# Output projection of a GLA layer on one NeuronCore: fourteen instead of ten weight pairs multiplied by seven block products, with the weight sums regrouped

## The chip, the cores and the metric

The kernel runs on one core of one Trainium2 chip. The metric is the device time of one launch in microseconds (us); lower is better. Three runs of the kernel before took 1044.53, 1044.98 and 1045.18 us (median 1044.98). A separate, profiled execution gives the trace that is read here.

The engines are named as the profile names them: PE is TensorE's matmul stream and PEld its weight loads, DVE is VectorE, ACT is ScalarE, POOL is GpSimd, SP issues most of the DMAs.

## What is computed

One layer with batch 1, 256 tokens, width 2048: RMSNorm, a gated linear attention mixer with four heads, a residual add, RMSNorm, a squared-ReLU MLP of width 8192, a residual add, and a last RMSNorm, all in float32.

```python
h = x
h = h + _gla_mixer(_rmsnorm(h, gla_norm), w_in, w_gate_up, b_gate, o_norm, w_out)
h = h + _sq_relu_mlp(_rmsnorm(h, mlp_norm), w_up, w_down)
return _rmsnorm(h, final_norm)

def _gla_mixer(...):
...
    return (o * silu(r)) @ w_out          # the output projection, 2048 x 2048

def _sq_relu_mlp(h, w_up, w_down):
    a = relu(h @ w_up)
    return (a * a) @ w_down
```

The change lies in the output projection (`@ w_out`) and, with the regrouped sums alone, in the second MLP matmul (`@ w_down`).

## The kernel before

**Precision by splitting.** PE multiplies in fp32r. Each float32 operand is therefore split into a part `hi` (an ACT cast, `copy_hi`, L112 to L118) and a remainder `lo = raw - hi` (a DVE subtraction, L131 for weights as loaded, L761 and L1129 for sums of weights). One block product is three matmuls: x_hi by w_hi, x_lo by w_hi, x_hi by w_lo.

**Steps of the output projection.** `out_group` (L699) runs four times, for g = 0 to 3, each for 512 of the 2048 output columns. A group takes eight steps, one for each pair kp of 128-row weight tiles (256 rows in all), in the order of `ORDER` (L782). The step's weights are four blocks of 128 by 256: row tile i, column half. The activations of the pair are four blocks A11, A12, A21, A22 of 128 tokens by 128 rows: the first digit is the half of the tokens, the second the row tile.

- A *plain* step multiplies all eight block pairs: 8 products of 3 matmuls, 24 matmuls of 256 columns (L748).
- A *summed* step uses Winograd's scheme with seven products, 21 matmuls: four with sums of activations S1 to S4 and with sums of weights, and the rest with the blocks themselves. Three products use weight blocks as loaded (L740, 9 matmuls, here called the step's *raw product*); four use sums or follow them (L762 to L765, 12 matmuls, the *sums product*). The sums product is held back as `pending` and runs one step later, after that step's own products (L749).

Which steps are summed: `summed(g)` (L784), in groups 0 and 3 the pairs 0 and 1, in groups 1 and 2 the pairs 0, 1 and 7, ten steps in all.

**What a summed step needs.** (1) The two row tiles are loaded by SP's queue (L729), and POOL's queue then adds the second block onto the first by an accumulating DMA (L730). (2) The raw product casts and splits only 768 of the 1024 columns (L733). (3) DVE forms the other sums in place by three subtractions or additions of 128 by 256 (L743 to L745), after the split of the same step. (4) The result is cast by ACT in two pieces of 512 columns (L758, recorded at L118) and split by DVE (L761). (5) The activations must be there in *forms*, the eight blocks S1 to S4 and A11 to A22 side by side: `turn_pair` (L600) builds them from transposed blocks, with `form_sums` (L591, three DVE operations, recorded at L606), one ACT cast of 1024 columns (L607) and one DVE split (L608). A pair without forms goes the plain way of `turn` (L628 to L630). `FORMED` (L596) names the pairs that get forms.

**Banks.** A group accumulates its plain results in two PSUM banks, `banks[0]` and `banks[1]`, one for each half of the tokens, which begin as a copy of h (`begin_out`, L669). The summed products go to two more banks, `p16` and `p57`, which are the same physical banks in every group. After the last summed step of a group (`final`), ACT copies both to SBUF (`comb`, L767 and L768), DVE combines them (L769 to L772), and at the end of the group DVE adds `comb` and the plain banks into h (L775). The next group's first matmul into `p16` starts that bank afresh, so it must wait for the copy of L767.

**Order on the engines.** `then_mm` (L692) keeps the products in the written order on PE: each block of matmuls is issued after the last matmul of the block before it. `issue_after` orders casts and splits likewise. In what remains, the tile scheduler chooses the order. Weights live in `raw` buffers (six) and in five pairs of `hi` and `lo` slots (`slots`, L120); the raw product and the sums product of a summed step each take a slot pair. A cast waits until PE has finished with the slot pair five uses earlier.

**Work between the steps.** `between` (L785 to L795) places other work after a step: after step 1 the transposes of the previous group's finished h (`turn`, L610; L616 on PE, L629 on ACT, L630 on DVE), after step 3 the opening copies of the next group (L673), after step 4 the sums of squares (L780). In group 0, step 1 carries the transposes of the attention output's pairs 4 to 7 instead.

**The MLP.** `down` (L1019) uses the same seven products for nearly all pairs of `w_down`, 112 summed steps, alternating on PE with plain steps of `w_up`. Its sums are at L1088 to L1090, its casts at L1121, its split at L1129; `early` and `late` (L1130, L1131) are the two halves of the sums product, with matmuls of `w_up` between them.

Of the kernel before, what the change touches and what calls it, by code (L numbers as in the profile page):

```python
# [30 lines left out]
ALU = mybir.AluOpType  # L31

P = 128
T = 256
# [12 lines left out]
G = 1024  # L47
GT = 512
# [11 lines left out]
OFF = 48  # L60
# [8 lines left out]
def tile_gla_mlp(ctx, tc, x, xt, cols, w_vg, w_in, w_gate, w_out, w_up, w_down, final_norm, out):  # L69
    nc = tc.nc  # L70
# [515 lines left out]
                nc.scalar.activation(s, acc[t][c], AF.Silu, scale=r1[:, t : t + 1])  # L586
                nc.vector.tensor_tensor(on[:, t, lo : lo + 512], on[:, t, lo : lo + 512], s, op=ALU.mult)

    S3, S1, S2, S4, A12, A11, A22, A21 = range(8)

    def form_sums(f, sub):  # L591
        sub(f[:, S3 : S1 + 1], f[:, A21:].to_broadcast([P, 2, P]), f[:, A11 : A22 + 1])
        sub(f[:, S2], f[:, A11], f[:, S1])
        sub(f[:, S4], f[:, A12], f[:, S2])

    FORMED = (0, 1, 7)  # L596
    in_forms = lambda a: a.rearrange("p (f s) -> p f s", f=8)
    raw_forms = [in_forms(some[:, 4:6].rearrange("p a b -> p (a b)")), in_forms(mid.tile([P, G], F32, tag="db", name="form"))]

    def turn_pair(kp, bank, gain, to):  # L600

        raw_form = raw_forms[kp == 1]
        for i in range(2):
            s = bank[:, i * T : (i + 1) * T].rearrange("p (t s) -> p t s", t=NT)
            nc.scalar.activation(raw_form[:, A12 + 1 - i :: 2], s, AF.Copy, scale=gain(2 * kp + i))
        form_sums(raw_form, lambda o, x, y: nc.vector.tensor_tensor(o, x, y, op=ALU.subtract))  # L606
        nc.scalar.copy(to[0], raw_form)  # L607
        nc.vector.tensor_tensor(to[1], raw_form, to[0].bitcast(F32), op=ALU.subtract)  # L608

# [30 lines left out]
    def forms_o(kp):  # L640
        if kp < 2:
            return [of_pairs[:, kp, i] for i in range(2)]
        return [a[:, OFF : OFF + G].rearrange("p (f s) -> p f s", f=8) for a in (oth, otl)]

    def place_o(kt):

# [52 lines left out]
    def out_group(g, order, summed, between):  # L699

        tt = nc.vector.tensor_tensor
        banks = [out_banks[g, t] for t in range(NT)]
        sums_banks = []
        begun = set()
        pending = None
        block = lambda i, n=1: slice(i * T, (i + n) * T)

        def product(bank, o, a, w, n, last=False):
            for x in a[: 2 - n]:
                for d in range(0, w.shape[-1], T):  # L710
                    newest[0] = nc.tensor.matmul(
                        bank[:, o + d : o + d + T], x, w[:, d : d + T],
                        start=bank in sums_banks and bank.name not in begun, stop=last, skip_group_check=True,
                    ).ins
                    begun.add(bank.name)

        def products(these, w, last=False):
            with then_mm():
                for n in range(2):
                    for bank, o, a, c in these:  # L720
                        product(bank, o, a, w[n][:, c], n, last and n == 1)

        for step, kp in enumerate(order):
            by = kp in summed
            raw = raw_tile()[:, : 2 * GT]
            src = w_out[2 * kp * P : 2 * (kp + 1) * P, g * GT : (g + 1) * GT].rearrange("(i p) c -> p i c", p=P)
            if by:
                for i in range(2):
                    last_load[0] = nc.sync.dma_start(out=raw[:, i * GT : (i + 1) * GT], in_=src[:, i])  # L729
                nc.gpsimd.dma_start(out=raw[:, :T], in_=src[:, 0, T:], accum_op=ALU.add)  # L730
            else:
                last_load[0] = nc.sync.dma_start(out=raw.rearrange("p (i c) -> p i c", i=2), in_=src)
            w = parts(raw, 2 * GT, slots(), [(T * by, 2 * GT)])  # L733
            if by:
                if not sums_banks:
                    sums_banks.extend(psum_bank(i) for i in out_ids[4:])
                f = forms_o(kp)
                at = lambda k, f=f: [a[:, k] for a in f]
                p16, p57 = sums_banks
                products([(p16, 0, at(A11), block(1)), (banks[0], T, at(A12), block(3)), (banks[0], 0, at(S4), block(2))], w)  # L740
                u = raw.rearrange("p (f s) -> p f s", f=4)
                with tc.issue_after(last_lo[0].ins):
                    tt(u[:, 2], u[:, 0], u[:, 2], op=ALU.add)  # L743
                    tt(u[:, 1], u[:, 2], u[:, 1], op=ALU.subtract)
                    last = tt(u[:, 3], u[:, 2], u[:, 3], op=ALU.add)  # L745
            else:
                for t, i in ((0, 0), (0, 1), (1, 0), (1, 1)):
                    products([(banks[t], 0, row_o(2 * kp + i, t), block(2 * i, 2))], w, step == len(order) - 1 and i == 1)  # L748
            if pending:  # L749
                pending()  # L750
                pending = None
            if step in between:
                with tc.issue_after(last_hi[0].ins), tc.issue_after(last_lo[0].ins), then_mm():
                    between[step]()
            if by:
                def pending(u=raw, at=at, final=kp == [k for k in order if k in summed][-1]):
                    to = slots()
                    for c in (0, GT):  # L758
                        copy_hi(to[0][:, c : c + GT], u[:, c : c + GT])
                    with tc.issue_after(last_lo[0].ins):  # L760
                        last_lo[0] = tt(to[1][:, :G], u, to[0][:, :G].bitcast(F32), op=ALU.subtract)  # L761
                    products([  # L762
                        (p57, 0, at(S1), block(0)), (p57, T, at(S3), block(1)),
                        (p16, T, at(S2), block(2)), (banks[1], T, at(A22), block(3)),
                    ], to, final)  # L765
                    if final:
                        nc.scalar.copy(comb[:, 1:3], two(p16))  # L767
                        nc.scalar.copy(comb[:, 0:4:3], two(p57))  # L768
                        tt(comb[:, 2], comb[:, 1], comb[:, 2], op=ALU.subtract)  # L769
                        tt(comb[:, 0], comb[:, 0], comb[:, 2], op=ALU.subtract)  # L770
                        tt(comb[:, 4], comb[:, 0], comb[:, 3], op=ALU.add)
                        tt(comb[:, 5], comb[:, 2], comb[:, 3], op=ALU.subtract)  # L772
        for t in range(NT):
            o = h[:, t, g * GT : (g + 1) * GT].rearrange("p (f s) -> p f s", f=2)
            tt(o, two(banks[t]), comb[:, 4 * t : 4 * t + 2], op=ALU.add)  # L775

    def ssq_h(g):
# [144 lines left out]
    def on_vector(i):  # L922
        newest_form[1] = i.ins
# [30 lines left out]
    def forms(m, kp, s):  # L954
# [2 lines left out]
            f[:, A12:].rearrange("p (t i) s -> p i t s", t=2), s.rearrange("p i (t s) -> p i t s", t=2), AF.Square  # L957
        ))
        if True in ways_of(m, kp):
            form_sums(f, lambda o, x, y: on_vector(nc.vector.tensor_tensor(o, x, y, op=ALU.subtract)))  # L960

    def form_parts(m, kp, act):
        ways = ways_of(m, kp)
# [55 lines left out]
    def down(passes):  # L1019
# [7 lines left out]
        for n, (m, g) in enumerate(passes):  # L1027
# [12 lines left out]
            for kp in range(KP):  # L1040
# [40 lines left out]
                if by_parts:  # L1081
                    these = (P16, 0, at(A11), block(1)), (B32, T, at(A12), block(3)), (B32, 0, at(S4), block(2))
                    u = raw.rearrange("p (f s) -> p f s", f=4)
                    tt = nc.vector.tensor_tensor


                    with tc.issue_after(last_lo[0].ins):
                        tt(u[:, 2], u[:, 0], u[:, 2], op=ALU.add)  # L1088
                        tt(u[:, 1], u[:, 2], u[:, 1], op=ALU.subtract)  # L1089
# [19 lines left out]
                def of_sums(u=raw, products=products, at=at, kp=kp, banks=banks, quick=fresh and quick, g=g, then=ahead_of):  # L1109
# [11 lines left out]
                    for c in (0, GT):  # L1121
                        copy_hi(to[0][:, c : c + GT], u[:, c : c + GT])
                    if quick and kp == 0:
                        settle(P57)
                        banks[BX4] = begin(BX4, g)
# [41 lines left out]
    def combine(g):  # L1167
# [4 lines left out]
        def put(t):  # L1172
# [1 line left out]
            nc.vector.tensor_tensor(hv, hv, e[:, :2], op=ALU.add)  # L1174

        return [
            tt(2, 1, 2, ALU.subtract), tt(0, 0, 2, ALU.subtract), lambda: put(0),
            tt(1, 2, 3, ALU.subtract), tt(0, 0, 3, ALU.add), lambda: put(1),
        ]

    passes = [(m, g) for m in range(ROUNDS) for g in order_of(m) if m < ROUNDS - 1 or g < 2]
# [130 lines left out]
```

## Time and profile before

| | before |
|---|---|
| runs, us | 1044.53, 1044.98, 1045.18 |
| the profiled execution: its time, us | 1045.44 |
| its span, first to last instruction, us | 1043.7 |
| matmuls on PE | 9064 |
| granted PE clock, mean | 0.998 |
| DVE / ACT / POOL busy, share of the span | 83% / 69% / 11% |
| output projection on PE (L711), us from the span's start | 288.1 to about 376.6 |
| DMA throughput, mean | 217 GB/s |

The profile's page gives busy time by engine, then groups of instructions. Instruction rows in a timeline are "start, duration, engine, line, operation, output<-inputs, shape, count", with the idle time of the engine before it and what ended that in brackets. A row with a count covers several instructions in sequence: its duration runs from the first start to the last end. Two facts matter for reading it. Matmuls overlap, so PE's speed is read from the distance between starts, not from the busy share. DVE and ACT instructions overlap by some tens of ns too, so what one costs in a dense sequence is again the distance between starts.

### The profile page before, as it was taken

How to read it: one execution, taken by the hardware profiler on the slowest of the kernel's cores; microseconds unless marked ns; L12 is line 12 of the kernel's file. 1: busy time of each engine (PE TensorE's matmuls, PEld its weight loads, DVE VectorE, ACT ScalarE, POOL GpSimd, SP SyncE). 2: the span in 40 equal slices, each digit the busy share in tenths (PEclk: the TensorE clock that was granted, in tenths of full speed). 3: DMA queues.
4: the chain of work that ended last, by engine and by line, in shares of the span. 5: the costliest groups of instructions: out<-in, count | busy, mean ns of one | idle time of the engine just before them, and what ended most of it. 6: DMA issues, size and time to landing. Idle time of an engine off the chain costs nothing. (4 is left out here: it accounts for less than half of the span.)

```text
span 1043.7 us, 23272 instructions
## 1 busy us (share of the span) xinstructions
PE 1035.2 (99%) x9064; PEld 1034.3 (99%) x9064; DVE 871.1 (83%) x1287; ACT 721.7 (69%) x1084; POOL 117.8 (11%) x161
## 2 busy tenths in 40 slices
PE   9999999999999999999999999999999999999997
PEld 9999999999999999999999999999999999999997
DVE  5768644656498866889999999999999999999887
ACT  6785544546477755678678688778778777777785
POOL 0000000010011001111111111111111111111100
PEclk9999999999999999999999999999999999999999
DMA  9957665556666686678887887887888888887782
GB/s 333 334 174 208 197 195 170 152 152 182 175 204 189 209 256 190 179 210 226 228 247 230 236 235 217 239 236 223 246 232 222 249 230 228 231 227 225 233 244 89
DMA packets 118414, 226.53 MB, mean 217 GB/s; under 512 B 10608, under 2 KB 26864, under 8 KB 118176
## 3 DMA queue, kind: packets, MB, share of 16 engines
q1 hardware_dynamic: 100064, 207.39, 63.5%
q0 software_dynamic: 17568, 16.00, 10.3%
q8 instruction: 71, 1.16, 0.4%
q10 hardware_dynamic: 672, 1.66, 0.4%
q14 instruction: 39, 0.32, 0.1%
HBM read 222.91 MB, written 2.10 MB: 216 GB/s over the span
## 5 line engine op out<-in xcount | busy, mean ns | idle before, releaser
L118 ACT CAST hi<-raw 128x512 fp32r<-128x512 f32 (+4 forms) x630 | 499.5, 835 | 263.0 <-DVE raw L1089 73.0
L131 DVE TENSOR_TENSOR lo<-raw,hi 128x768 fp32r<-128x768 f32 (+3 forms) x226 | 238.7, 1061 | 90.9 <-ACT hi L118 88.4
L855 PE MATMUL acc<-hi,act 128*128 128x256 f32 x1696 | 247.9, 276 | 0.0
L855 PE MATMUL up<-hh,hi 128*128 128x256 f32 x1024 | 238.8, 277 | 0.0
L855 PE MATMUL up<-hl,hi 128*128 128x256 f32 x1024 | 238.7, 276 | 0.0
L165 DVE TENSOR_TENSOR lo<-raw,hi 128x1024 fp32r<-128x1024 f32 x160 | 195.0, 1221 | 29.9 <-ACT hi L118 29.5
L855 PEld LDWEIGHTS acc<-hi,act 128*128 128x128 f32 x1696 | 217.7, 188 | 0.0
L855 PEld LDWEIGHTS up<-hl,hi 128*128 128x128 f32 x1024 | 192.3, 188 | 0.0
L855 PEld LDWEIGHTS up<-hh,hi 128*128 128x128 f32 x1024 | 192.3, 188 | 0.0
L1065 POOL DMA_DIRECT2D raw<-in_w_down x112 | 97.1, 867 | 518.6 <-DMA raw<-in_w_down 229.8
L1129 DVE TENSOR_TENSOR lo<-raw,hi 128x1024 fp32r<-128x1024 f32 x112 | 136.7, 1220 | 1.3 <-ACT hi L118 1.0
L855 PE MATMUL up<-hh,lo 128*128 128x256 f32 x1024 | 137.0, 276 | 0.0
L855 PE MATMUL acc<-lo,act 128*128 128x256 f32 x848 | 134.1, 276 | 0.0
L855 PEld LDWEIGHTS up<-hh,lo 128*128 128x128 f32 x1024 | 125.7, 188 | 0.0
L855 PEld LDWEIGHTS acc<-lo,act 128*128 128x128 f32 x848 | 113.5, 188 | 0.0
L176 PE MATMUL acc<-hi,xA 128*128 128x256 f32 (+1 forms) x728 | 105.5, 279 | 0.2
L176 PEld LDWEIGHTS acc<-hi,xA 128*128 128x128 f32 x728 | 93.8, 188 | 0.7 <-ACT hi L118 0.6
L176 PE MATMUL acc<-lo,xA 128*128 128x256 f32 (+1 forms) x364 | 60.9, 278 | 0.1
L176 PEld LDWEIGHTS acc<-lo,xA 128*128 128x128 f32 x364 | 50.3, 188 | 0.3 <-DVE lo L131 0.3
L1088 DVE TENSOR_TENSOR raw<-raw 128x256 f32<-128x256 f32 x112 | 47.5, 424 | 2.9
L1089 DVE TENSOR_TENSOR raw<-raw 128x256 f32<-128x256 f32 x112 | 47.5, 424 | 2.8
L219 PE MATMUL acc<-xA,hi 128*128 128x256 f32 x288 | 49.2, 276 | 0.0
(185 smaller groups left out, 1281.9 us busy)
## 6 DMA issues: line engine op xcount, KB each, us to landing
raw<-in_w_up SPq DMA_DIRECT2D x128, 512.0 KB, 4.6
raw<-in_w_down SPq DMA_DIRECT2D x224, 256.0 KB, 4.4
raw<-in_w_in SPq DMA_DIRECT2D x80, 512.0 KB, 3.7
raw<-in_w_down POOLq DMA_DIRECT2D x112, 128.0 KB, 5.1
raw<-in_w_out SPq DMA_DIRECT2D x22, 512.0 KB, 4.7
raw<-in_w_down SPq DMA_DIRECT2D x16, 512.0 KB, 4.8
raw<-in_w_vg SPq DMA_DIRECT2D x14, 520.0 KB, 8.4
raw<-in_w_out SPq DMA_DIRECT2D x20, 256.0 KB, 3.4
```

The source lines that it names most:

```text
L118: last_hi[0] = nc.scalar.copy(to, raw)
L131: last_lo[0] = nc.vector.tensor_tensor(lo[:, s], raw[:, s], hi[:, s].bitcast(F32), op=ALU.subtract)
L165: last_lo[0] = nc.vector.tensor_tensor(to[1], dst, to[0].bitcast(F32), op=ALU.subtract)
L176: nc.tensor.matmul(o[:, m], x, w[:, m], start=first and c == 0, stop=last, skip_group_check=True)
L219: nc.tensor.matmul(o, u[:, i, s], m, start=kt == 0 and n == 0 and j % 2 == 0, stop=kt == KT - 1 and n == 2, skip_group_check=True,)
L855: newest[0] = nc.tensor.matmul(o, x, w, start=first, stop=last, skip_group_check=True).ins
L1065: nc.gpsimd.dma_start(out=raw[:, :T], in_=src[:, 0, T:], accum_op=ALU.add)
L1088: tt(u[:, 2], u[:, 0], u[:, 2], op=ALU.add)
L1089: tt(u[:, 1], u[:, 2], u[:, 1], op=ALU.subtract)
L1129: last_lo[0] = nc.vector.tensor_tensor(to[1][:, :G], u, to[0][:, :G].bitcast(F32), op=ALU.subtract)
```

## The change

- `FORMED` becomes (0, 1, 6, 7). Groups 0 and 1 sum pairs 0, 1 and 7; groups 2 and 3 sum all four. That is 3 + 3 + 4 + 4 = 14 summed steps for 10.
- Groups 2 and 3 get another order of pairs: 0, 3, 2, 1, 7, 4, 6, 5. In these groups the first step is a summed one, and the last summed step (pair 6) is the seventh of eight, so its sums product is the group's last work on PE.
- Pair 6 gets forms in group 0 (`turn_pair` for it as well as for pair 7), with a raw buffer of its own.
- The seven-product scheme is rewritten with other signs. The form sums remain three DVE operations. The weight sums become two: one of 128 by 256, and one of 128 by 512 that takes the first one's result from blocks 1 and 3 at once. Blocks 0 and 2 are then cast first, and blocks 1 and 3 second, where before it was 0 and 1, then 2 and 3.
- The order of the four products in the sums product changes from S1, S3, S2, A22 to S1, S2, S3, A22; in the MLP, `early` is now S1 and S2, `late` S3 and A22.
- The combining operations get other signs, at the same count.

```diff
-    S3, S1, S2, S4, A12, A11, A22, A21 = range(8)
-
-    def form_sums(f, sub):
-        sub(f[:, S3 : S1 + 1], f[:, A21:].to_broadcast([P, 2, P]), f[:, A11 : A22 + 1])
-        sub(f[:, S2], f[:, A11], f[:, S1])
-        sub(f[:, S4], f[:, A12], f[:, S2])
-
-    FORMED = (0, 1, 7)
+    S3, S2, S1, S4, A12, A11, A22, A21 = range(8)
+
+    def form_sums(f, tt):
+        tt(f[:, S3], f[:, A21], f[:, A11], ALU.subtract)
+        tt(f[:, S2 : S1 + 1], f[:, A22 : A22 + 1].to_broadcast([P, 2, P]), f[:, 0::7], ALU.add)
+        tt(f[:, S4], f[:, A12], f[:, S2], ALU.subtract)
+
+    def weight_sums(u):
+        nc.vector.tensor_tensor(u[:, 2], u[:, 0], u[:, 2], op=ALU.subtract)
+        return nc.vector.tensor_tensor(u[:, 1::2], u[:, 1::2], u[:, 2:3].to_broadcast([P, 2, T]), op=ALU.subtract)
+
+    FORMED = (0, 1, 6, 7)
...
-        raw_form = raw_forms[kp == 1]
+        raw_form = raw_forms[kp % 2]
...
-        return [a[:, OFF : OFF + G].rearrange("p (f s) -> p f s", f=8) for a in (oth, otl)]
+        c = (12 * T + OFF + 128, OFF)[kp - 6]
+        return [in_forms(a[:, c : c + G]) for a in (oth, otl)]
...
-                    tt(u[:, 2], u[:, 0], u[:, 2], op=ALU.add)
-                    tt(u[:, 1], u[:, 2], u[:, 1], op=ALU.subtract)
-                    last = tt(u[:, 3], u[:, 2], u[:, 3], op=ALU.add)
+                    weight_sums(u)
...
-                    for c in (0, GT):
-                        copy_hi(to[0][:, c : c + GT], u[:, c : c + GT])
+                    for a in range(2):
+                        copy_hi(*(x.rearrange("p (f s) -> p f s", f=4)[:, a::2] for x in (to[0][:, :G], u)))
...
-                        (p57, 0, at(S1), block(0)), (p57, T, at(S3), block(1)),
-                        (p16, T, at(S2), block(2)), (banks[1], T, at(A22), block(3)),
+                        (p57, 0, at(S1), block(0)), (p16, T, at(S2), block(2)),
+                        (p57, T, at(S3), block(1)), (banks[1], T, at(A22), block(3)),
...
-    ORDER = (3, 0, 2, 1, 4, 7, 5, 6)
+    ORDER = (3, 0, 2, 1, 4, 7, 5, 6), (0, 3, 2, 1, 7, 4, 6, 5)
+    summed = lambda g: FORMED if g > 1 else (0, 1, 7)
     newest[0] = None
-    summed = lambda g: FORMED if 0 < g < GROUPS - 1 else FORMED[:2]
-    out_group(0, ORDER, summed(0), {
+    out_group(0, ORDER[0], summed(0), {
...
-        out_group(g, ORDER, summed(g), {
+        out_group(g, ORDER[g > 1], summed(g), {
...
-                        tt(u[:, 2], u[:, 0], u[:, 2], op=ALU.add)
-                        tt(u[:, 1], u[:, 2], u[:, 1], op=ALU.subtract)
-                        last_sum[0] = tt(u[:, 3], u[:, 2], u[:, 3], op=ALU.add).ins
+                        last_sum[0] = weight_sums(u).ins
...
-                    early = (P57, 0, at(S1), block(0)), (P57, T, at(S3), block(1))
-                    late = (P16, T, at(S2), block(2)), (BX4, T, at(A22), block(3))
+                    early = (P57, 0, at(S1), block(0)), (P16, T, at(S2), block(2))
+                    late = (P57, T, at(S3), block(1)), (BX4, T, at(A22), block(3))
```

More of the change, by code (lines that the diff above doesn't have):

```diff
@@ L605, in turn_pair @@
             nc.scalar.activation(raw_form[:, A12 + 1 - i :: 2], s, AF.Copy, scale=gain(2 * kp + i))
-        form_sums(raw_form, lambda o, x, y: nc.vector.tensor_tensor(o, x, y, op=ALU.subtract))
+        form_sums(raw_form, lambda o, x, y, op: nc.vector.tensor_tensor(o, x, y, op=op))
         nc.scalar.copy(to[0], raw_form)
@@ L768, in pending @@
                         nc.scalar.copy(comb[:, 0:4:3], two(p57))
-                        tt(comb[:, 2], comb[:, 1], comb[:, 2], op=ALU.subtract)
+                        tt(comb[:, 2], comb[:, 1], comb[:, 2], op=ALU.add)
                         tt(comb[:, 0], comb[:, 0], comb[:, 2], op=ALU.subtract)
-                        tt(comb[:, 4], comb[:, 0], comb[:, 3], op=ALU.add)
-                        tt(comb[:, 5], comb[:, 2], comb[:, 3], op=ALU.subtract)
+                        tt(comb[:, 4], comb[:, 0], comb[:, 3], op=ALU.subtract)
+                        tt(comb[:, 5], comb[:, 2], comb[:, 3], op=ALU.add)
         for t in range(NT):
@@ L959, in forms @@
         if True in ways_of(m, kp):
-            form_sums(f, lambda o, x, y: on_vector(nc.vector.tensor_tensor(o, x, y, op=ALU.subtract)))
+            form_sums(f, lambda o, x, y, op: on_vector(nc.vector.tensor_tensor(o, x, y, op=op)))
     def form_parts(m, kp, act):
@@ L1083, in down @@
                     u = raw.rearrange("p (f s) -> p f s", f=4)
-                    tt = nc.vector.tensor_tensor
                     with tc.issue_after(last_lo[0].ins):
-                        tt(u[:, 2], u[:, 0], u[:, 2], op=ALU.add)
-                        tt(u[:, 1], u[:, 2], u[:, 1], op=ALU.subtract)
-                        last_sum[0] = tt(u[:, 3], u[:, 2], u[:, 3], op=ALU.add).ins
+                        last_sum[0] = weight_sums(u).ins
                 else:
@@ L1120, in of_sums @@
                         ahead = {k: begin(k, then[1]) for k in (B32, P16)}
-                    for c in (0, GT):
-                        copy_hi(to[0][:, c : c + GT], u[:, c : c + GT])
+                    for a in range(2):
+                        copy_hi(*(x.rearrange("p (f s) -> p f s", f=4)[:, a::2] for x in (to[0][:, :G], u)))
                     if quick and kp == 0:
@@ L1176, in combine @@
         return [
-            tt(2, 1, 2, ALU.subtract), tt(0, 0, 2, ALU.subtract), lambda: put(0),
-            tt(1, 2, 3, ALU.subtract), tt(0, 0, 3, ALU.add), lambda: put(1),
+            tt(2, 1, 2, ALU.add), tt(0, 0, 2, ALU.subtract), lambda: put(0),
+            tt(1, 2, 3, ALU.add), tt(0, 0, 3, ALU.subtract), lambda: put(1),
         ]
```

## The prediction

> **What bounds the kernel now.** First the page's line of engines, then PE's own rows in the output projection (a timeline, and the first and last starts of its matmul line), because a busy PE need not be a PE at its peak.
>
> ```profile
> span 1043.7 us, 23272 instructions
> ...
> PE 1035.2 (99%) x9064; PEld 1034.3 (99%) x9064; DVE 871.1 (83%) x1287; ACT 721.7 (69%) x1084; POOL 117.8 (11%) x161
> ```
>
> ```profile
> 290.87 0.84 PE L711 MATMUL acc<-hi,of 128*128 128x256 f32 x6
> 291.55 0.51 PE L711 MATMUL acc<-lo,of 128*128 128x256 f32 x3
> 291.89 1.91 PE L616 MATMUL aux<-ident,on 128*128 128x128 f32 x16
> 293.56 0.48 PE L711 MATMUL acc<-hi,oth 128*128 128x256 f32 x2
> ```
>
> ```profile
> L711 PE MATMUL acc<-hi,oth x190: 275/276/364, 288.1 to 375.9; 128*128 128x256 f32 x190
> ...
> L711 PE MATMUL acc<-lo,oth x190: 275/276/284, 288.6 to 376.4; 128*128 128x256 f32 x190
> ```
>
> Six matmuls start between 290.87 and 291.55, so one takes 0.1133 us. Sixteen transposes start between 291.89 and 293.56: 0.104 us each. By the code the projection has 4 x 8 x 24 - 10 x 3 = 738 matmuls and 40 transposes among them (16 in group 0, 8 in each other group). 738 x 0.1133 + 40 x 0.104 = 87.8 us; from 288.1 to the last start at 376.4 plus one matmul there are 88.4. So at most about 0.6 us of this stage is PE waiting: here PE's issue rate is the bound, and an edit gains only what it takes off PE. The rest of the engines decide whether PE stays fed. How close they are is in the four group windows of the projection and one window of the MLP (columns: window, length, then PE, PEld, DVE, ACT, POOL busy).
>
> ```profile
> 288.00:311.00 23.00, 23.00 (x205) 23.00 (x204) 21.58 (x36) 16.99 (x28) 2.62 (x3) 1.00 0.66 189
> 311.00:333.00 22.00, 22.00 (x196) 22.00 (x196) 19.08 (x29) 15.89 (x27) 2.64 (x3) 1.00 0.71 201
> 333.00:355.00 22.00, 22.00 (x196) 22.00 (x195) 19.54 (x32) 15.76 (x27) 1.76 (x2) 1.00 0.73 211
> 355.00:377.00 22.00, 22.00 (x196) 22.00 (x195) 18.68 (x27) 13.85 (x22) 0.00 (x0) 1.00 0.78 256
> ...
> 900.00:920.00 20.00, 20.00 (x179) 20.00 (x179) 19.86 (x31) 13.80 (x20) 3.46 (x4) 1.00 0.93 247
> ```
>
> DVE is the next engine: 21.58 of 23 us in group 0, and nearly full in that MLP window, where PE nevertheless starts as many matmuls per us as elsewhere (179 touch the 20 us, 196 the 22). It works ahead of PE, and how far is read from the time at which a split ends and PE first uses it. The narrowest place of group 0 is pair 7 in step 5, of group 2 pair 5 in step 6:
>
> ```profile
> 298.35 2.35 DVE L131 TENSOR_TENSOR lo<-raw,hi 128x1024 fp32r<-128x1024 f32 x2
> ...
> 342.78 1.22 DVE L131 TENSOR_TENSOR lo<-raw,hi 128x1024 fp32r<-128x1024 f32 x1
> ```
>
> ```profile
> 303.35 0.39 PE L711 MATMUL acc<-lo,oth 128*128 128x256 f32 x2
> ...
> 348.10 0.39 PE L711 MATMUL acc<-lo,oth 128*128 128x256 f32 x2
> ```
>
> The first of the two splits at 298.35 ends at 298.35 + 1.22 = 299.57 and is used at 303.35: 3.8 us ahead. The one at 342.78 ends at 344.00, used at 348.10: 4.1 us ahead. These 3.8 us are the cover of everything that follows.
>
> **What the change takes off PE.** Four steps go from 24 to 21 matmuls: 12 x 0.1133 = **-1.36 us**. Nothing else leaves PE; the MLP keeps its matmuls. This is also the most that the change can gain, but for the 0.6 us above.
>
> **What it adds to DVE.** The prices are distances between starts in a dense piece at the end of group 2; it is needed again below.
>
> ```profile
> 353.14 0.42 DVE L769 TENSOR_TENSOR some<-some 128x256 f32<-128x256 f32 x1 [0.45 <-ACT some L767]
> 353.60 0.42 DVE L770 TENSOR_TENSOR some<-some 128x256 f32<-128x256 f32 x1
> 353.94 0.42 DVE L772 TENSOR_TENSOR some<-some 128x256 f32<-128x256 f32 x1
> 354.28 1.22 DVE L761 TENSOR_TENSOR lo<-raw,hi 128x1024 fp32r<-128x1024 f32 x1
> 355.41 0.42 DVE L771 TENSOR_TENSOR some<-some 128x256 f32<-128x256 f32 x1
> 355.75 0.68 DVE L775 TENSOR_TENSOR h<-acc,some 128x512 f32<-128x512 f32 x1
> 356.35 0.95 DVE L131 TENSOR_TENSOR lo<-raw,hi 128x768 fp32r<-128x768 f32 x1
> 357.21 0.69 DVE L775 TENSOR_TENSOR h<-acc,some 128x512 f32<-128x512 f32 x1
> ```
>
> 256 elements cost 0.34 us (353.60 to 353.94), 0.46 where the next operation needs the result (353.14 to 353.60), 512 cost 0.60, 768 cost 0.86, 1024 cost 1.13. Three weight sums were 0.46 + 0.34 + 0.34 = 1.14; two are 0.46 + 0.60 = 1.06, so -0.08 a summed step. A step that becomes summed pays 0.86 + 1.06 + 1.13 for 1.13 before: +1.92. The forms of pair 6 are priced by those of pair 7:
>
> ```profile
> 296.96 0.28 DVE L606 TENSOR_TENSOR some<-some 128x128 f32<-128x128 f32 x1
> 297.17 1.26 DVE L630 SCALAR_TENSOR_TENSOR otl<-aux,colt,oth 128x256 fp32r<-128x256 f32 x3
> ...
> 300.61 1.22 DVE L608 TENSOR_TENSOR otl<-some,oth 128x1024 fp32r<-128x1024 f32 x1
> ```
>
> 0.21 (296.96 to 297.17) + 0.46 + 0.28 for the three sums and 1.13 for the split, less two plain remainders of 0.42 that it replaces (three in 1.26): +1.24. By group: group 0, 1.92 - 0.16 + 1.24 = +3.00; group 1, -0.24; group 2, 1.92 - 0.24 = +1.68; group 3, 3.84 - 0.16 = +3.68; together +8.1. Set against the windows, each shortened by 0.34 us per step newly summed: group 0 has 24.6 us of DVE work in 22.7, group 1 18.8 in 22.0, group 2 21.2 in 21.7, group 3 22.4 in 21.3. The whole is 87.0 in 87.6. So DVE falls back by 1.9 us in group 0, recovers in group 1, and falls back by about 1 in group 3, where the MLP's opening steps need no sums. Both are under the 3.8 us of cover, so I cost the DVE work at **0**; without the cover it costs PE up to 8.1 - 3.8 = 4.3 us. The bounds are 0 and 4.3; I take 0 because the lag computed is 1.9.
>
> ACT gets, for each new summed step, a cast of 768 and one of 1024 columns for one of 1024, and for pair 6 one more cast of 1024. From the rows below a cast of 1024 is at most 1.05 us, so 5 x 1.05 = 5.3 us at most in windows that leave 6 to 8 us idle each: 0. POOL issues four more accumulating DMAs; its line in this projection reads
>
> ```profile
> L730 POOL DMA_DIRECT2D raw<-in_w_out x10: 872/875/1033, 269.8 to 347.9; - x10
> ```
>
> so 0.88 us each on an engine with 2.6 us of work in a window; each now stands in the queue behind one more load and one more accumulation. With six raw buffers the loads run that many steps ahead, some 15 us: 0. The next thing late would be the first weight sum, and behind it the cast of the sums product on ACT.
>
> **What the new order moves.** Three covers go at the start of group 3. Group 2's sums product of pair 6 is now its last PE work, and group 3 begins with pair 0's raw product, whose first matmul opens bank `p16` again. Before, a plain step ended group 2 and another opened group 3. So PE now waits for ACT's copy of `p16`. ACT's and PE's rows there, before:
>
> ```profile
> 352.04 0.58 ACT L768 COPY some<-acc 128x512 f32<-128x512 f32 x1
> 352.52 0.59 ACT L767 COPY some<-acc 128x512 f32<-128x512 f32 x1
> ...
> 357.18 1.05 ACT L118 CAST hi<-raw 128x1024 fp32r<-128x1024 f32 x1 [1.88 <-PE acc L711]
> ```
>
> ```profile
> 354.44 0.39 PE L711 MATMUL acc<-hi,oth 128*128 128x256 f32 x2
> ...
> 357.16 0.84 PE L711 MATMUL acc<-hi,of 128*128 128x256 f32 x6
> 357.84 0.51 PE L711 MATMUL acc<-lo,of 128*128 128x256 f32 x3
> 358.19 1.04 PE L616 MATMUL aux<-ident,h 128*128 128x128 f32 x8
> ```
>
> The handover from PE to ACT: the cast at 357.18 follows the last matmul of the step before, which started at 357.16 - 0.11 = 357.05, so 0.13 us after its start. From ACT to the next engine: the copy ends at 352.52 + 0.59 = 353.11 and DVE begins at 353.14, 0.03. Let U be the start of the group's last matmul. The new product order puts the last write of `p16` two matmuls before it, at U - 0.23. The copy runs from U - 0.10 to U + 0.49, PE can go on at U + 0.52 instead of U + 0.11: **+0.41 us**. Lower bound 0: the raw product has six matmuls into `banks[0]`, 0.68 us, which cover it if the scheduler puts them ahead (it did place L768 ahead of L767, and L772 ahead of L771, against the written order). Upper bound: `p57` first, 0.48 to 0.6 more, and a cast of 1.05 ahead of both: 2.06. I take 0.41, since PE's rows show the written order in every step, and ACT's last cast before that point is due one step earlier.
>
> [...] No row of this projection shows PE waiting in such a place.
>
> The second cover: the transposes of group 2's h run after step 1 of group 3. Before, they began at 358.19, and the second add into h ended at 357.21 + 0.69 = 357.90, 0.29 us earlier. Now the combining, which was done during the last step, starts only after U. Copies end at U + 0.96, the four operations at U + 2.1, two adds of 0.60 at U + 3.4; with two splits in between, as in the rows above (1.13 and 0.86), U + 5.4. The transposes are due after 9 + 24 + 12 matmuls, 5.10 us, that is at U + 0.11 + 0.41 + 5.10 = U + 5.62. One more split or pair of sums in between makes them 0.9 late. Bounds 0 and 0.9; I take **+0.2**, because DVE is fuller than it was.
>
> Third, the same combining at the end of group 3. h is needed by the squares in the MLP's first steps, later than before by the copies and the combining, U + 2.1; PE uses it only for pair 6 of the first w_up pass, and casts there are as far ahead as above: 0.
>
> **The MLP.** 112 steps lose 0.08 us of DVE each, and the cast of blocks 0 and 2 needs only the first sum. ACT is the one that waited there:
>
> ```profile
> L118 ACT CAST hi<-raw 128x512 fp32r<-128x512 f32 (+4 forms) x630 | 499.5, 835 | 263.0 <-DVE raw L1089 73.0
> ```
>
> But PE did not wait for ACT, so shorter waits gain 0; they raise the cover. The last sum ends 0.46 + 0.69 = 1.15 after the first one's start, against 0.46 + 0.34 + 0.42 = 1.22, so nothing becomes later. Should the new order of `early` and `late` delay something, its cover is the w_up matmuls between them.
>
> **Sum.** -1.36 + 0.41 + 0.2 = -0.75. Against the profiled execution (1045.44, span 1043.7, so 1.74 around it) that is 1044.69; that execution lies 0.46 above the median of the runs, so on the median's scale 1044.98 - 0.75 = **1044.2**.
>
> **The rivals.**
> *All covered* (the six matmuls go first, the adds are in time): -1.36, 1043.6. For it: the reordering seen on ACT and DVE. Against it: PE's rows follow the written order.
> *DVE becomes the bound in the projection, slower.* The place is groups 0 and 3. It decides from the point at which DVE is over 3.8 us behind. Its idle time before was 10 us of 89, mostly waits for casts; if these waits stay, all 8.1 us added count and 4.3 reach PE: -1.36 + 0.61 + 4.3 = +3.6, 1048.5. For it: 87.0 of 87.6 us. Against it: the windows' overruns are at most 1.9.
> *The turn of group 2 to 3 at its upper bounds*: -1.36 + 2.06 + 0.9 = +1.6, 1046.6. For it: a cast of 1.05 us in front of the copies needs only one order of the scheduler's. Against it: that cast is due later than the copies.
> *The change doesn't do what it says*: PE would still show 9064 matmuls and 1045.0; nothing speaks for it.
>
> **How the numbers follow.** Forecast 0.53 (its own range 1043.7 to 1045.0), all covered 0.25, DVE bound 0.11, the turn at its upper bounds 0.08, others 0.03. Within 0.2% means within 2.1 us of 1044.98, 1042.9 to 1047.1; about that is what a measurement can tell from no change. Forecast, covered and turn all lie within; the DVE case lies over it where it has its full price. Faster 0.05, same 0.83, slower 0.12. The range, 1043.2 to 1046.8, reaches from the covered case less the runs' own spread (0.4) to the turn's upper bound with 0.2 to spare, and leaves out the DVE case at full price.
>
> **What would show it right or wrong.** PE has 9052 matmuls and the projection is shorter by 0.7 to 1.4 us. At its turn from group 2 to 3, one distance between starts of about 0.5 instead of 0.113 us before the raw product of pair 0, or its `banks[0]` matmuls ahead. At most a short one before the transposes of group 3. DVE busy above 21 us in the windows of groups 0, 2 and 3, but splits still over 1 us ahead of their use. The weight sums show 112 operations of 256 and 112 of 512 elements at about 0.42 and 0.69 us. The forecast is wrong if PE's rows show gaps anywhere else, if a 512-element sum takes much over 0.69 us, or if the MLP's part grows.

## The result, and the profile after

The changed kernel takes 1055.8 us (median of four runs, 1054.79 to 1056.48) against 1044.78 for the kernel before in the same comparison: ratio 1.0103, 95% interval 1.0087 to 1.0119. It is slower by 1%, where 0.07% faster was forecast, and far outside the range given. The profiled execution took 1055.93, with a span of 1053.5 us, 9.8 longer.

The page of the changed kernel, engines, and the trace's rows for the two new weight sums (duration: least, median, most):

```profile
span 1053.5 us, 23161 instructions
...
PE 1039.0 (99%) x9052; PEld 1035.5 (98%) x9052; DVE 868.6 (82%) x1179; ACT 737.0 (70%) x1093; POOL 121.3 (12%) x165
```

```profile
L597 DVE TENSOR_TENSOR raw<-raw x126: 411/424/427, 282.0 to 1015.9; 128x256 f32<-128x256 f32 x126
...
L598 DVE TENSOR_TENSOR raw<-raw x126: 677/692/694, 282.4 to 1016.3; 128x512 f32<-128x512 f32 x126
```

The change does what it says: 12 matmuls fewer, and sums of 0.42 and 0.69 us (126 of each, 112 in the MLP and 14 in the projection). The MLP is not where the time went. From the end of the first sixteen w_up steps to the last matmul both traces have 614.9 us. From the first matmul of the output projection to the last start in those sixteen steps, in what follows *the stage*, there are 133.2 us before and 142.9 after. Group by group, with one window for the start of the MLP (columns as in the prediction's windows):

```profile
288.00:311.00 23.00, 23.00 (x206) 23.00 (x205) 20.40 (x30) 17.75 (x28) 1.74 (x2) 1.00 0.48 130
311.00:335.00 24.00, 22.78 (x195) 22.14 (x194) 18.94 (x31) 14.76 (x26) 2.63 (x3) 1.00 0.68 197
335.00:359.00 24.00, 22.95 (x191) 22.21 (x190) 19.86 (x29) 15.30 (x28) 4.37 (x5) 1.00 0.68 196
359.00:384.00 25.00, 23.48 (x193) 22.55 (x192) 20.83 (x30) 17.74 (x30) 0.87 (x1) 1.00 0.61 185
384.00:399.00 15.00, 13.11 (x110) 12.77 (x110) 11.62 (x18) 6.88 (x13) 1.08 (x2) 1.00 1.00 368
```

In group 0 PE is busy throughout; from group 1 on it is not, and yet DVE is busy for only 79 to 83% of groups 1 to 3 (85 to 89% before) and ACT for 62 to 71%. Nobody is full: the engines wait for each other. The sums product of pair 7 in group 1 shows how. PE's timeline:

```profile
328.35 0.28 PE L716 MATMUL acc<-hi,oth 128*128 128x256 f32 x1
328.47 0.28 PE L716 MATMUL acc<-hi,otl 128*128 128x256 f32 x1
328.58 0.28 PE L716 MATMUL acc<-hi,oth 128*128 128x256 f32 x1
328.69 0.28 PE L716 MATMUL acc<-hi,otl 128*128 128x256 f32 x1
329.67 0.39 PE L716 MATMUL acc<-hi,oth 128*128 128x256 f32 x1 [0.70 <-ACT hi L118]
...
330.12 0.28 PE L716 MATMUL acc<-hi,otl 128*128 128x256 f32 x1
330.93 0.74 PE L716 MATMUL acc<-lo,oth 128*128 128x256 f32 x4 [0.52 <-DVE lo L764]
```

After four matmuls with S1 and S2, which need the first half cast, PE waits for the second half (0.98 us between starts instead of 0.11), and after four more for the split (0.81). DVE's timeline there, and ACT's five casts between 325.84 and 329.61, each from a window of its own, since the timeline merges casts in sequence:

```profile
325.35 0.42 DVE L597 TENSOR_TENSOR raw<-raw 128x256 f32<-128x256 f32 x1
325.80 0.69 DVE L598 TENSOR_TENSOR raw<-raw 128x512 f32<-128x512 f32 x1
329.64 1.23 DVE L764 TENSOR_TENSOR lo<-raw,hi 128x1024 fp32r<-128x1024 f32 x1 [3.15 <-ACT hi L118]
330.79 3.22 DVE L131 TENSOR_TENSOR lo<-raw,hi 128x1024 fp32r<-128x1024 f32 x3
```

```profile
325.84 0.62 ACT L118 CAST hi<-raw 128x512 fp32r<-128x512 f32 x1 [2.29 <-PE acc L716]
326.37 1.04 ACT L118 CAST hi<-raw 128x1024 fp32r<-128x1024 f32 x1
327.32 0.83 ACT L118 CAST hi<-raw 128x768 fp32r<-128x768 f32 x1
328.05 1.04 ACT L118 CAST hi<-raw 128x1024 fp32r<-128x1024 f32 x1
329.00 0.61 ACT L118 CAST hi<-raw 128x512 fp32r<-128x512 f32 x1
```

ACT works from 325.84 to 329.61 without a pause. Two of the casts are the halves of this step's sums (512 columns); between them stand three casts for later products (1024, 768 and 1024 columns). The sums are ready at 325.80 + 0.69 = 326.49, the second half is cast at 329.6. DVE's next instruction is the split, which needs both halves, so DVE stands for 3.15 us, although the three splits behind it (in a row at 330.79) have had their casts since 327.41, 328.15 and 329.09.

The second place is the start of the MLP, where PE waits for the row sums of 1/rms (L821), and behind them for everything:

```profile
395.38 0.28 PE L858 MATMUL up<-hl,hi 128*128 128x256 f32 x1
397.55 0.92 PE L821 MATMUL row<-work,ones 128*128 128x128 f32 x4 [1.90 <-DVE work L813]
```

```profile
391.07 0.68 DVE L778 TENSOR_TENSOR h<-acc,some 128x512 f32<-128x512 f32 x1
392.07 1.22 DVE L165 TENSOR_TENSOR lo<-raw,hi 128x1024 fp32r<-128x1024 f32 x1 [0.31 <-ACT hi L118]
393.21 0.68 DVE L778 TENSOR_TENSOR h<-acc,some 128x512 f32<-128x512 f32 x1
394.93 1.23 DVE L165 TENSOR_TENSOR lo<-raw,hi 128x1024 fp32r<-128x1024 f32 x1 [1.04 <-ACT hi L118]
396.08 0.16 DVE L806 TENSOR_REDUCE ms<-hs 128x2 f32<-128x8 f32 x1
```

The last add into h comes at 393.21, and the squares, their sum (396.08), the power and the diagonals follow in a chain.

The third part is not a wait at all. In these windows PE is busy throughout, yet 87 matmuls touch the 10 us of one and 90 those of the other:

```profile
350.00:360.00 10.00, 10.00 (x87) 10.00 (x86) 7.76 (x11) 4.34 (x8) 1.74 (x2) 1.00 0.76 246
400.00:410.00 10.00, 10.00 (x90) 10.00 (x89) 5.74 (x8) 4.99 (x7) 0.00 (x0) 1.00 0.42 121
```

Starts are 117.8 ns apart in the first and 113.3 in the second, at the same granted clock (1.00). Added up over the stage's starts, against the kernel before: -1.36 us of matmuls, +9.3 us of waits (every distance over 125 ns, less 113), +1.7 us of the wider spacing. That is 9.6 of the 9.7 us by which the stage grew.

### The profile page after: what moved, and what is told of

It reads as the page before. It is cut to its first block, busy times and chain, and to the rows that moved or that the text cites. A ratio compares the mean times of both kernels' runs of the same rounds, so it can differ in the third digit from the quotient of the medians.

```text
span 1053.5 us, 23161 instructions
## 1 busy us (share of the span) xinstructions
PE 1039.0 (99%) x9052; PEld 1035.5 (98%) x9052; DVE 868.6 (82%) x1179; ACT 737.0 (70%) x1093; POOL 121.3 (12%) x165
## 4 chain that ended last, share of the span: by engine, by line
PE 90%; issue 4%; DMA 2%; DVE 1%; ACT 1%; SPq 0%; POOL 0%; POOLq 0%; DVEq 0%; ACTq 0%
PE up L858 32%; PE acc L858 27%; PE acc L176 17%; PE acc L219 6%; PE acc L716 3%; PE aux L219 2%; DMA raw<-in_w_vg 2%; ACT hi L118 1%; DMA raw<-in_w_out 1%; DVE lo L131 1%; PE aux L176 1%; PE aux L521 1%; PE aux L620 1%; ACT sqf L1198 0%; DVE lo L764 0%
## 5 line engine op out<-in xcount | busy, mean ns | idle before, releaser
L118 ACT CAST hi<-raw 128x512 fp32r<-128x512 f32 (+4 forms) x638 | 511.2, 832 | 228.3 <-PE acc L176 64.5
L598 DVE TENSOR_TENSOR raw<-raw 128x512 f32<-128x512 f32 x126 | 86.9, 690 | 3.1
L597 DVE TENSOR_TENSOR raw<-raw 128x256 f32<-128x256 f32 x126 | 53.2, 422 | 2.8
```

The lines of the kernel that those rows point to most:

```text
L118: last_hi[0] = nc.scalar.copy(to, raw)
L597: nc.vector.tensor_tensor(u[:, 2], u[:, 0], u[:, 2], op=ALU.subtract)
L598: return nc.vector.tensor_tensor(u[:, 1::2], u[:, 1::2], u[:, 2:3].to_broadcast([P, 2, T]), op=ALU.subtract)
```

## The experiments

Theory A: the casts between the halves starve PE; the rest is the combining at a group's end. Rivals: B, fourteen steps are too much work for DVE and ACT in any order; C, the new sums or the strided half casts cost time themselves. "Waits" and "spacing" are what the stage has more of than the kernel before. Each set of runs had runs of the kernel before beside it, with medians of 1044.78 to 1045.05 us; a ratio is to those of its own set.

| run | steps | median, us | ratio to before (95%) | stage, us | waits | spacing |
|---|---|---|---|---|---|---|
| before | 10 | 1044.78 | | 133.2 | | |
| after | 14 | 1055.8 | 1.0103 (1.0087 to 1.0119) | 142.9 | 9.3 | 1.7 |
| one_cast | 14 | 1046.79 | 1.0017 (1.0007 to 1.0026) | 134.8 | 2.1 | 0.8 |
| halves01 | 14 | 1046.96 | 1.0020 (1.0010 to 1.0030) | 134.9 | 2.2 | 0.8 |
| sums_ten | 10 | 1045.25 | 1.0002 (0.9992 to 1.0011) | 133.2 | 0 | 0 |
| steps_old | 14 | 1060.61 | 1.0151 (1.0135 to 1.0166) | 148.0 | 14.0 | 2.1 |
| in_order | 14 | 1048.53 | 1.0041 (1.0024 to 1.0058) | 135.6 | 3.8 | 0 |
| one_cast_13 | 13 | 1044.87 | 0.9999 (0.9990 to 1.0008) | 133.1 | 0.9 | 0 |
| one_cast_12 | 12 | 1044.32 | 0.9994 (0.9985 to 1.0003) | 132.5 | 0 | 0 |
| one_cast_end | 14 | 1047.23 | 1.0020 (1.0011 to 1.0029) | 135.0 | 2.2 | 1.0 |
| pinned_end | 14 | 1046.12 | 1.0012 (1.0003 to 1.0021) | 134.1 | 0.8 | 1.5 |

In the traces, other weight casts stand between the two halves in 12 of the changed kernel's 14 sums, in 11 of 14 in steps_old, in none of halves01 and sums_ten, and in one of in_order (the last, two casts of w_up).

**One cast for the sums (one_cast).**

```diff
-                    for a in range(2):
-                        copy_hi(*(x.rearrange("p (f s) -> p f s", f=4)[:, a::2] for x in (to[0][:, :G], u)))
+                    copy_hi(to[0][:, :G], u)
```

> The changed kernel, but in the output projection the sums of a step are cast in one piece of 1024 columns, so that no other cast can stand between the two halves. Theory A (in the changed kernel ACT puts one to three other casts between the two half casts, DVE's split of the sums stands waiting at the head of DVE's queue, and PE runs dry): the gaps of 0.7 and 0.8 us before and within the sums products go, 7.2 us in all, and with them the slower matmul starts after them; the wait of 2.2 us before the row sums at the start of the MLP stays. 1045.5 to 1047. Theory B (DVE and ACT have too much work in fourteen steps, whatever the order): gaps stay, 1052 or more.

1046.8, as A said. DVE's rows at the same place:

```profile
323.31 0.42 DVE L597 TENSOR_TENSOR raw<-raw 128x256 f32<-128x256 f32 x1
323.77 0.69 DVE L598 TENSOR_TENSOR raw<-raw 128x512 f32<-128x512 f32 x1
325.62 1.23 DVE L763 TENSOR_TENSOR lo<-raw,hi 128x1024 fp32r<-128x1024 f32 x1 [1.17 <-ACT hi L118]
```

The wait before the split is one cast long (1.17 us), not 3.15, and PE passes this product without a gap. So one instruction in place of two gives back some nine of the eleven us. With it theory B falls: with the casts set otherwise the same fourteen steps leave PE 2.1 us of waits instead of 9.3. What stays are 1.35 us around pair 1 in group 3 and 0.75 before the row sums.

**Half casts as before the change (halves01).**

```diff
-                    for a in range(2):
-                        copy_hi(*(x.rearrange("p (f s) -> p f s", f=4)[:, a::2] for x in (to[0][:, :G], u)))
+                    for c in (0, GT):
+                        copy_hi(to[0][:, c : c + GT], u[:, c : c + GT])
```

> The changed kernel with two half casts in the output projection again, but as before the change, blocks 0 and 1, then 2 and 3; both need the second sum, so in the built order they stand together nearly everywhere. Theory A: as with one cast, 1045.5 to 1047.5. Theory B: 1052 or more. Theory C (the split by blocks 0 and 2, with its strided rows, is what costs time): also quick, but then the run with ten steps and the new casts is slow.

1047.0. Two halves are no worse than one cast when they stand together, and here all fourteen pairs do. By the code both halves need the second sum; that this keeps them together is argued, not tested.

**The new sums and casts alone (sums_ten).**

```diff
-    FORMED = (0, 1, 6, 7)
+    FORMED = (0, 1, 7)
...
-    ORDER = (3, 0, 2, 1, 4, 7, 5, 6), (0, 3, 2, 1, 7, 4, 6, 5)
-    summed = lambda g: FORMED if g > 1 else (0, 1, 7)
+    ORDER = (3, 0, 2, 1, 4, 7, 5, 6), (3, 0, 2, 1, 4, 7, 5, 6)
+    summed = lambda g: FORMED if 0 < g < GROUPS - 1 else FORMED[:2]
```

> Ten steps in the old order and with the old forms, but with the new sums and the new half casts in projection and MLP. In the built order the two halves stand together in nearly all steps. Theory A: no gaps, 1044.5 to 1045.2, the same as before. Theory C (the new sums or strided casts cost time themselves): several us slower, with gaps before sums products or in the MLP.

1045.25, not to be told from before, and no gap. C falls: neither the sums nor the strided casts cost anything, here or in the MLP. The scheduler sets no other weight cast between the halves in any of these ten steps.

**The steps alone (steps_old).** The kernel before with the changed kernel's `FORMED`, `ORDER`, `summed`, `forms_o` and `raw_forms`, and its own three sums and half casts.

> Fourteen steps in the new order, with the forms of pair 6, but with the old three sums and the old half casts (blocks 0 and 1, then 2 and 3), in projection and MLP. In the built order other casts stand between the halves in most steps. Theory A: slow, 1052 to 1057, with gaps in the sums products and the wait before the row sums. Theory C: 1046 or less.

1060.6, slower than expected and than the whole change. So the fourteen steps in the new order are enough for the scheduler to set other casts between the halves, with the old sums too. They aren't enough whichever the halves: in halves01 the same steps leave them together. Whether the number of steps or their order does it, no run separates. Here PE is busy for 4.94 of 7 us, and 3 us at half the granted clock follow (the column after POOL's, 0.50). Of the 14.0 us in the table some 1.4 are matmuls at that clock (an estimate: 13 touch the 2.90 busy us and would take 1.47 at 113.3 ns each):

```profile
326.00:333.00 7.00, 4.94 (x41) 4.54 (x39) 3.43 (x7) 3.77 (x5) 0.89 (x1) 0.98 0.51 150
333.00:336.00 3.00, 2.90 (x13) 2.90 (x14) 3.00 (x4) 1.07 (x2) 0.00 (x0) 0.50 0.80 135
```

**The order alone (in_order).** The changed kernel with every weight cast of the projection issued after the one written before it:

```diff
     newest[0] = None
+    ordered[0] = True
     out_group(0, ORDER[0], summed(0), {
...
+    ordered[0] = False
     r2 = const.tile([P, NT], F32, name="r2")
```

> The changed kernel with its half casts of blocks 0 and 2, then 1 and 3, but all weight casts of the projection pinned to the written order on ACT, so that no cast of weights stands between two halves. Nothing else differs. Theory A (the casts between the halves are the cause): near the run with one cast, 1046 to 1048. Theory D (two casts instead of one are what ACT cannot carry in fourteen steps): 1052 or more, like the changed kernel.

This is the sharpest test, since the work is that of the changed kernel: PE, DVE and ACT run as many instructions as there (9052, 1179, 1093). All gaps in sums products are gone. Two waits are left, 1.40 us between starts in the transposes of group 3 and 2.24 before the row sums. The median of 1048.53 is over the expected 1048, the profiled run with 1047.98 is not: the ten runs spread from 1047.15 to 1057.36 us, the five longest, from 1049.07 on, at a mean granted clock of 0.996 to 0.997 instead of 0.998 to 0.999. What lengthens those, no trace here shows. PE's and DVE's rows at the first wait:

```profile
358.63 0.38 PE L620 MATMUL aux<-ident,h 128*128 128x128 f32 x2
360.14 0.87 PE L620 MATMUL aux<-ident,h 128*128 128x128 f32 x6 [1.13 <-DVE h L778]
```

```profile
355.33 1.22 DVE L764 TENSOR_TENSOR lo<-raw,hi 128x1024 fp32r<-128x1024 f32 x1
356.46 0.42 DVE L774 TENSOR_TENSOR some<-some 128x256 f32<-128x256 f32 x1
356.80 0.68 DVE L778 TENSOR_TENSOR h<-acc,some 128x512 f32<-128x512 f32 x1
357.40 2.08 DVE L131 TENSOR_TENSOR lo<-raw,hi 128x1024 fp32r<-128x1024 f32 x2
359.40 0.69 DVE L778 TENSOR_TENSOR h<-acc,some 128x512 f32<-128x512 f32 x1
```

One split stands ahead of the last combining operation (L774) and two more (one row, 357.40) between the adds into h; the second add ends at 360.09.

**Fewer steps (one_cast_13, one_cast_12), and an earlier end (one_cast_end).**

```diff
 one_cast_13
+    summed = lambda g: FORMED if g == 2 else (0, 1, 7)
 one_cast_12
+    FORMED = (0, 1, 7)
+    summed = lambda g: FORMED
 one_cast_end
+    ORDER = (3, 0, 2, 1, 4, 7, 5, 6), (0, 3, 2, 1, 7, 4, 6, 5), (0, 3, 1, 2, 7, 6, 4, 5)
```

All three have the one cast of one_cast. Group 3 of one_cast_13 and all groups of one_cast_12 have the old order; the last order in one_cast_end is that of group 3.

> One cast, and thirteen summed steps: group 3 sums pairs 0, 1 and 7 in the old order, so its last sums product is followed by a plain step, and it begins with a plain one. Theory A with its second part (what is left, 1.35 us of gaps in group 3 and 0.75 before the row sums, comes from group 3's four summed steps and from combining after the last matmul): both go; 9 matmuls less than before, 1.02 us; 1043.8 to 1044.6. Rival (the gaps belong to the four sums of group 2): 1045 or more.

> One cast, and twelve summed steps: pairs 0, 1 and 7 in every group, the old order, no forms for pair 6. Theory A: no gaps; 6 matmuls less, 0.68 us; 1044.2 to 1044.8. Rival (new sums or one cast cost something of their own in this stage): 1045 or more.

> One cast and fourteen steps, with group 3 in the order 0, 3, 1, 2, 7, 6, 4, 5, so that two plain steps follow its last summed one. Theory A, second part: the 0.75 us before the row sums go, the gaps in group 3 stay or grow, since its sums stand closer together: 1045.5 to 1047. Rival (the row sums wait for something else): the 0.75 us stay.

Twelve steps leave no gap, and the stage is shorter by 0.68 us, just the 6 matmuls; the best median of all, 1044.32, though its interval still holds 1. With thirteen the gaps in group 3 go, but 0.84 us before the row sums stay: expected wrongly, and 1044.87 lies between what theory A and its rival said. There DVE's second diagonal (L812) stands behind a split of w_up:

```profile
385.80 0.29 DVE L812 TENSOR_SCALAR work<-ident,r 128x128 f32<-128x128 f32 x1 [0.68 <-POOL r L356]
386.29 1.23 DVE L165 TENSOR_TENSOR lo<-raw,hi 128x1024 fp32r<-128x1024 f32 x1 [0.20 <-ACT hi L118]
387.44 0.28 DVE L812 TENSOR_SCALAR work<-ident,r 128x128 f32<-128x128 f32 x1
```

So in that small wait DVE's order has a part again. In one_cast_end it is gone, and group 3's gaps have grown, to one of 1.6 us, where three summed pairs stand close together; 1047.23 is a little over the expected 1047.

**Order pinned and an earlier end (pinned_end).** in_order with 0, 3, 1, 2, 7, 6, 4, 5 for groups 2 and 3.

> The changed kernel with weight casts pinned to the written order on ACT, and groups 2 and 3 in the order 0, 3, 1, 2, 7, 6, 4, 5, so that two plain steps follow the last summed one. Theory A, second part (the 1.4 us before group 3's transposes and the 2.2 us before the row sums come from combining after the group's last matmul): both go. If its sums, three pairs close together, leave no gap: 1043.5 to 1044.3, otherwise a gap before the sums products of pairs 7 and 6. Rival (they come from DVE's and ACT's load as a whole): both waits stay, 1046.5 or more.

Both waits of in_order are gone; 0.8 us of short gaps and 1.5 of wider spacing remain, so the run isn't quick. Moving the combining away from the group's last matmul thus removes both waits, though one_cast_13, whose group 3 ends with a plain step, shows that splits of w_up in DVE's queue can keep part of the second. A fourteen-step version quicker than before was not found.

**Four transposes in the first projection (reset, reset_12).** Four transposes of the identity on PE near 46 us, in the kernel before and in one_cast_12. The later matmuls of that projection are issued behind them, so the edit also pins an order.

> The kernel before, with four transposes of the identity (results unused) on PE near the end of the first projection, about 45 us from the start, where matmuls start 117.8 ns apart. In the profiles so far, matmuls start 117.8 ns apart from a wait of PE on, and 113.3 ns apart again after the next transposes. Theory E (the transposes themselves bring the closer spacing back): from about 48 us on 113.3 ns, some 12 us of work quicker by 4%, 0.5 us, less 0.4 us for the transposes: 1044.6 to 1045.1, shown by the spacing alone. Rival (it is something else around 60 us, such as the loads' end): spacing stays 117.8 until 62 us.

> The same four transposes in the kernel with twelve summed steps and one cast. 1044.0 to 1044.6, as without them or 0.1 less; shows whether the quickest version can be told from the kernel before.

Theory E, that transposes end the wider spacing wherever they stand, falls. Spacing is as wide behind the transposes at 46 us as ahead of them (three starts in 0.35 to 0.36 us on both sides, from 44.28 and from 47.37). Worse, it is still wide from 62 to 152 us, where 257 matmuls touch each 30 us; in the kernel before it ends at 64. That it would go on beyond 62 us neither theory nor rival foresaw. Both kernels lose some 4 us, 1049.19 (ratio 1.0040, 1.0026 to 1.0054) and 1048.43 (1.0032, 1.0021 to 1.0044). Thirty us of the same projections, first in reset, then before:

```profile
92.00:122.00 30.00, 30.00 (x257) 30.00 (x256) 21.99 (x37) 16.85 (x18) 0.30 (x3) 1.00 0.66 194
```

```profile
96.00:126.00 30.00, 30.00 (x267) 30.00 (x267) 21.52 (x38) 18.21 (x23) 2.33 (x16) 1.00 0.68 196
```

## Why the prediction was wrong

- **PE's share, -1.36 us: right.** In one_cast_12 six matmuls fewer make the stage 0.68 us shorter, 0.113 each.
- **The step that failed is the cost of the new work on DVE and ACT, put at 0.** DVE's lag was worked out from sums of work (87.0 us in 87.6), and ACT's casts were laid into its idle time, with the sums of a step priced as one cast of 1024 columns where the code makes two of 512. What counted was which instruction stood at the head of DVE's queue, since it held those behind it: with the half casts torn apart, DVE stood for up to 3.15 us per sums product with ready splits behind, the 3.8 us of cover were used up in group 1, and PE waited 7 us in groups 1 to 3. in_order shows it: same work, same sums, no such waits. The rival "DVE becomes the bound" had the direction, by way of waits for casts, but not the place (groups 0 and 3, where PE waits in 1 to 3 and not in 0), the size (+3.6 where it was +11.0) or the reason: DVE was less busy per us than before.
- **The opening of `p16`, +0.41: it cost 0, the lower bound.** The scheduler did put other matmuls ahead (ten, by these rows: the six into `banks[0]`, four of the plain step), and the three into `p16` start only at 359.69. `then_mm` holds a block only behind the matmul written last in the block before, and the three written first were moved behind that. ACT's copy of `p16` ran from 358.48 to 359.07, that is from U + 0.08 with U = 358.40, later than the U - 0.10 of the prediction, and was still covered:

```profile
358.05 0.63 PE L716 MATMUL acc<-lo,oth 128*128 128x256 f32 x4
358.52 0.63 PE L716 MATMUL acc<-hi,of 128*128 128x256 f32 x4
358.99 0.40 PE L716 MATMUL acc<-lo,of 128*128 128x256 f32 x2
359.22 0.40 PE L716 MATMUL acc<-hi,oth 128*128 128x256 f32 x2
359.46 0.40 PE L716 MATMUL acc<-hi,otl 128*128 128x256 f32 x2
359.69 0.40 PE L716 MATMUL acc<-hi,of 128*128 128x256 f32 x2
```

  The order was changed in the built program, and PE's starts in these rows go on without a wait, two in 0.23 to 0.24 us. So no run here shows what the 0.41 took for granted, that a matmul which waits for its bank holds those behind it.
- **The transposes of group 3, +0.2: mis-sized.** In the changed kernel nothing, as PE itself was late; in in_order 1.40 us between starts, 1.29 more than without a wait and beyond the upper bound of 0.9. The mechanism of that bound is what happened, three splits among the combining and the adds in place of two. But the bound also had PE 0.41 late at `p16`, and it wasn't: U was 353.41, the transposes were due at U + 5.21 and began at 358.63, and 0.9 + 0.41 is 1.3.
- **The end of group 3, put at 0: wrong.** The argument looked at pair 6 of w_up as the user of h, and overlooked that the row sums hang on the same h by way of the squares and are set earlier in PE's order. In the changed kernel PE waits 2.2 us before them; with one cast, the same end of the group costs 0.75.
- **The MLP, 0: right.** 614.9 us in both traces, and sums_ten at 1045.25.
- The spacing of matmul starts was taken as fixed; it cost 1.7 us that no step named.

## What to carry to other kernels

When an engine gets more work, don't stop at its sum: ask for the head of its queue, as with DVE here, where one split kept three ready ones waiting for up to 3.15 us, above all where one instruction needs two results that a scheduler may set apart. An operation cut in two so that its first half can start early must be pinned, or the gap between the halves can be filled with work that isn't urgent. And where a group's last work changes, follow its result to every user, the small side chains too.

## What the runs showed of the hardware

Two spacings of matmul starts were seen for the same 128x128 by 128x256 product at a granted clock of 1.00: 113.3 and 117.8 ns. In reset the wider one is there from 62 to 152 us: 257 matmuls touch each 30 us, and 266 to 268 each 30 us from 66 to 156 in the kernel before. By an estimate from the two spacings, some 764 starts in these 90 us cost 4.5 ns more each, 3.4 us of the 3.9 by which the span of reset is longer (1047.6 against 1043.7). The wider spacing began after waits of PE in mid-product (0.98 and 0.81 us between starts from 328.69 and 330.12 in the changed kernel, then 117 to 119 ns from 332.29 on), but starts were also wider right behind transposes with no wait before them (in the kernel before, 113 ns ahead of the row sums and transposes from 388.26 on, and 118 to 121 from 389.70 to 390.90). It ended soon after some stretches of transposes (in the changed kernel 118 ns ahead of the row sums and transposes from 397.55 on, and 113 again from 400.61), but not after those added in reset; in in_order, waits before transposes (1.40 us) or row sums (2.24 us) added no spacing to the stage (0 in the table), and 193 matmuls touch the 21.87 busy us of its window 354 to 377, where 196 touch 22. What sets it is open. And 7 us with PE busy for 4.94 were followed by 3 us at half the granted clock (0.50) in steps_old; a single wait of 2.17 us before the row sums of the changed kernel, or 0.98 and 0.81 us within 3, were not (1.00 in its windows 320 to 340 and 390 to 410).
